# State space parameters made in the first stage, and the modulation's shift as a bias per column, in a hybrid S5 and gated DeltaNet block

## The chip, the cores and the metric

One core of a Trainium2 chip runs the whole kernel. The metric is the device time of one execution in microseconds (us), the median of several runs. The engines are named as in the profile: PE (TensorE), DVE (VectorE), ACT (ScalarE), POOL (GpSimd) and SP (SyncE), whose queue issues nearly all DMAs here.

## What is computed

The input x has 2048 tokens of 1024 columns. One conditioning vector c gives shift, scale and gate; the modulated and normalised h goes through one projection of 3088 columns, whose column groups feed a state space branch (u and z_a), a gated DeltaNet branch (q, k, v, z_b) and the DeltaNet's decay and step sizes (beta and alpha, called AB in the kernel).

```python
mod = silu(c) @ ada_w + ada_b
shift, scale, gate = split(mod, 3)
h = rms_norm(x, norm_w) * (1 + scale) + shift
u, z_a, qkv, z_b, beta, alpha = split(h @ w_in)
# state space branch: two directions, 32 groups of 64 states and 16 channels
dt = exp(log_step); mag = exp(lam_re * dt)
ab = mag * (cos(lam_im * dt), sin(lam_im * dt))   # one step of the recurrence
f = (ab - 1) / lam; bb = f * b                    # the input matrix
y_a = glu(gelu(scan(ab, bb, c, u) + d * u)) * silu(z_a)
# DeltaNet branch: convolution of five taps, chunks, two directions
y_b = norm(delta(silu(conv(qkv)), beta, alpha)) * silu(z_b)
out = rms_norm(x + gate * (concat(y_a, y_b) @ w_out))
```

What depends on lam and log_step alone (the powers of ab, f, and the turning factors of the scan) needs neither the input matrix b nor the output matrix c of the state space; those are the parameters of which the title speaks.

## The kernel before

**Numbers.** The projection runs in fp16 with split operands: each weight tile is scaled by a power of two and cut in a high half wh and a low half wl, h likewise in hhi and hlo, and a gemm of one tile of 128 columns by 512 tokens is 24 matmuls (eight slices k of the 1024 rows, in each hi by hi, hi by lo, lo by hi). `w_max` finds a weight tile's scale (squares on ACT, a sum over partitions by one matmul), `w_cut` applies it (three small operations on the DVE, wh on ACT, wl on the DVE). PSUM has eight banks: two named gm for gemms, three named pt and three named sq for turned (transposed) h and for small sums.

**First stage** (lines 250 to 497, an order written by hand). It loads x in four blocks of 512 tokens and the modulation's weights ada_w, makes h and the four tiles of u, and the gate. Loads go through SP's one queue in program order: c, ada_b, norm_w, the first weights (ws), x, then ada_w. The DVE sums the modulation (acc, with slices aw of ada_w), a matmul with ones (`mod_sum`) finishes it: first for the scale, later for the shift, last for the gate (accg). For a block, `x_square` (ACT), `x_root` (DVE) and `x_scale` normalise x, `h_turn` turns a slice k of it on PE into a bank, and `h_part` makes h of it:

```python
A.activation(out=hf, in_=src, func=AF.Identity, scale=aS[:, k:k + 1], bias=shS[:, k:k + 1])
P.tensor_scalar(out=hhi[:, k, sl], in0=hf, scalar1=1.0, scalar2=1.0, op0=ALU.mult, op1=ALU.mult)
V.tensor_tensor(out=hlo[:, k, sl], in0=hf, in1=hhi[:, k, sl], op=ALU.subtract)
```

Since the shift is known late, h of block 0 is first made without it, with a scale of its own (s_0, ih0); a chain of 96 matmuls of one column then multiplies the shift with the u weights (ub), and u of block 0 gets this as a bias. Blocks 1 to 3 wait for the shift, and h of block 0 is made again with the shift during block 3, for the later jobs. Block by block, four gemms (`u_out`, ct = 0 to 3) go with the work for the next block: scaling after the first, h after the third and fourth.

**Job stage.** The other 21 column tiles are jobs in a fixed order (`order`): three tiles of z_a, AB, K, Q, then V mixed with the rest. A job has four ticks (AB one), in each the gemm of one block, what leaves the bank (Silu for z, a copy into raw for the convolutions), a piece of the next job's `w_max` and `w_cut`, delayed work by ticks (`later`: the taps of the convolution, squares, turns) and one step of the generator `side`. That generator is the state space branch: parameters (`s5_params`, 9 steps), tables of input and output matrices per group (24), a reordering through DRAM, turning factors, the main loop over 16 batches (33), and the opening of the GLU: 85 steps in all, over the 81 ticks and some more at the end. The parameters are rows loaded by DMA, turned on PE, then some 250 small operations on the DVE (exponential, sine and cosine, the f, powers by doubling, squares, and the tables rtA and rtB) and a product with b on POOL.

**DeltaNet stages.** After the jobs comes the DeltaNet in two stages with the GLU beside it and the output projection at the end, in an order written by hand. The change doesn't touch them.

## Time and profile before

| what | value |
|---|---|
| median of 3 runs | 1407.08 us (1400.67 to 1408.08) |
| the profiled execution, its own time | 1399.43 us |
| its span | 1397.7 us |
| mean granted PE clock | 0.963 of full speed |
| first gemm starts | 40.18 us |
| block 2's first gemm starts | 112.25 us |
| job 4, the first of the job stage, starts | 165.66 us |
| end of the job stage, start of DeltaNet and GLU | about 770 us |

A row of the timeline reads: start in us, duration in us, engine, line, operation, written tile and read tiles, sizes, how many alike, and in brackets the idle time ahead of it on this engine with what ended it. A row of a table by windows reads: the window, its length, then for PE, PEld (weight loads), DVE, ACT and POOL the busy time with the count of instructions, then the granted PE clock, the busy share of the DMA engines and GB/s. A row of the waits reads: engine, tile and line, what it waited for, then total us, how often, the longest.

### The profile page before, as it was taken

Reading aid. Unit: us, or ns where it says so; the run is one execution under the profiler, and the core shown is the slowest. Engines: PE = TensorE matmul, PEld = TensorE weight load, DVE = VectorE, ACT = ScalarE, POOL = GpSimd, SP = SyncE. Lnnn points to the kernel's source line nnn. Section 1 sums busy time; section 2 is a strip of 40 time slices with the busy share of each in tenths; the row PEclk is TensorE's granted clock in tenths of the full one; section 3 lists DMA queues with packets and bytes.
Section 4 is the critical chain, followed back from the end, with each engine's and each line's share of the span. In section 5 each row is a group of like instructions: output and inputs, shape, how many; then the busy total and the mean of one; then the engine's idle time right before and its main releaser. Section 6 shows DMA issues by size and latency. Waiting matters only on the chain.

```text
span 1397.7 us, 26524 instructions
## 1 busy us (share of the span) xinstructions
PE 1282.3 (92%) x9936; PEld 900.3 (64%) x9936; DVE 1017.6 (73%) x2095; ACT 672.5 (48%) x1348; POOL 708.1 (51%) x680
## 2 busy tenths in 40 slices
PE   2879897898999999999999699999999988998997
PEld 2445343355665555555554588999998877887885
DVE  4635579877765899998984667888878655865664
ACT  4445322444655454354445566776667423432332
POOL 3214223656540477878840766666553235654443
PEclk9789999999999999999999899999999999999998
DMA  9446343223457434343524533544335488686533
GB/s 308 173 86 187 92 87 87 64 82 89 121 163 191 132 106 129 99 143 95 156 80 135 163 83 96 175 144 143 115 132 184 150 294 279 223 312 211 181 107 112
DMA packets 255280, 206.43 MB, mean 148 GB/s; under 512 B 88496, under 2 KB 206256, under 8 KB 255152
## 3 DMA queue, kind: packets, MB, share of 16 engines
q1 hardware_dynamic: 255152, 204.75, 47.3%
q8 instruction: 78, 1.28, 0.4%
q14 instruction: 50, 0.41, 0.1%
HBM read 133.38 MB, written 73.33 MB: 148 GB/s over the span
## 4 chain that ended last, share of the span: by engine, by line
PE 67%; DVE 16%; DMA 4%; issue 3%; POOL 3%; ACT 2%; SPq 1%; DVEq 0%; POOLq 0%; ACTq 0%
PE gm L33 37%; PE sq L33 15%; PE pt L33 12%; DVE sq L1033 2%; DVE w L510 2%; DVE tm L510 1%; DVE xs L939 1%; PE pt L1077 1%; POOL w L510 1%; DMA y<-ya_d 1%; DVE t L510 1%; PE sq L1750 1%; DMA xt<-in_x_dram 0%; DVE r L1782 0%; DVE cv L1033 0%
## 5 line engine op out<-in xcount | busy, mean ns | idle before, releaser
L33 PE MATMUL gm<-hhi,wh 128*128 128x512 f16 (+1 forms) x784 | 294.4, 390 | 13.4 <-ACT wh L221 6.9
L33 PE MATMUL gm<-hhi,wl 128*128 128x512 f16 (+1 forms) x784 | 293.1, 388 | 8.2 <-DVE wl L223 8.2
L33 PE MATMUL gm<-hlo,wh 128*128 128x512 f16 (+1 forms) x784 | 293.4, 389 | 0.0
L33 PEld LDWEIGHTS <-wh 128*128 128x128 f16 (+1 forms) x1664 | 154.0, 100 | 199.7 <-issue 26.0
L33 PEld LDWEIGHTS <-wl 128*128 128x128 f16 (+1 forms) x832 | 79.8, 100 | 106.1 <-DVE wl L223 10.7
L1017 ACT ACTIVATE raw<-gm,w 128x512 f32<-128x512 f32 x48 | 33.1, 689 | 175.9 <-PE gm L33 175.9
L510 POOL TENSOR_TENSOR w<-w,w 128x512 f32<-128x512 f32 x32 | 50.2, 1578 | 87.9 <-DVE w L510 87.9
L33 PE MATMUL gm<-yh,gwh 128*128 128x256 f32 x256 | 80.0, 313 | 6.7 <-ACT yh L778 5.6
L1033 DVE SCALAR_TENSOR_TENSOR sq<-raw,cw,cv 128x512 f32<-128x512 f32 x48 | 55.2, 1151 | 29.6 <-ACT cv L1025 29.5
L1033 DVE SCALAR_TENSOR_TENSOR sq<-raw,cw,sq 128x512 f32<-128x512 f32 x96 | 72.6, 756 | 3.4
L33 PE MATMUL gm<-yl,gwh 128*128 128x256 f32 x256 | 73.3, 286 | 0.7 <-POOL yl L779 0.7
L1772 POOL TENSOR_TENSOR r<-r,xt 128x512 f32<-128x512 f32 x32 | 41.5, 1297 | 62.9 <-DVE r L1771 29.2
L33 PE MATMUL gm<-yh,gwl 128*128 128x256 f32 x256 | 72.5, 283 | 0.0
L1442 ACT ACTIVATE Y<-pt 128x512 f16<-128x512 f32 x96 | 58.0, 604 | 23.9 <-PE pt L33 23.2
L33 PE MATMUL sq<-S,kq 128*128 128x128 f32 x480 | 62.3, 281 | 0.0
L939 DVE TENSOR_TENSOR_SCAN xs<-c,w 128x255 f32<-128x255 f32 x64 | 61.1, 1013 | 1.1 <-POOL w L510 1.1
L33 PEld LDWEIGHTS sq<-S,kq 128*128 128x128 f32 x480 | 59.9, 196 | 2.0
L1421 DVE CAST_PREDICATED pb<-msk,pt 128x512 f16<-128x512 int8 x80 | 56.9, 714 | 5.5 <-PE pt L33 4.4
L1003 ACT ACTIVATE z<-gm,w 128x512 f32<-128x512 f32 x32 | 22.0, 688 | 80.0 <-PE gm L33 48.0
L33 PE MATMUL pt<-Y,nh 128*128 128x64 f16 (+1 forms) x896 | 56.3, 198 | 4.5 <-DVE Y L1429 4.2
L320 POOL TENSOR_SCALAR hhi<-hf 128x512 f16<-128x512 f32 x32 | 30.1, 960 | 54.9 <-ACT hf L318 47.9
L1443 ACT ACTIVATE YT<-pt 128x512 f16<-128x512 f32 x96 | 57.3, 597 | 0.0
(455 smaller groups left out, 3544.9 us busy)
## 6 DMA issues: line engine op xcount, KB each, us to landing
xt<-in_x_dram SPq DMA_DIRECT2D x25, 512.0 KB
ws<-in_w_in_dram SPq DMA_DIRECT2D x24, 512.0 KB
aw<-in_ada_w_dram SPq DMA_DIRECT2D x24, 512.0 KB
kq<-kT_d SPq DMA_DIRECT2D x32, 256.0 KB
kq<-qT_d SPq DMA_DIRECT2D x32, 256.0 KB
kt<-kt_d SPq DMA_DIRECT2D x32, 256.0 KB
vt<-vt_d SPq DMA_DIRECT2D x32, 256.0 KB
out_dram<-r SPq DMA_DIRECT2D x16, 512.0 KB
```

Source lines behind the costliest of these rows:

```text
L33: nc.tensor.matmul(out, lhsT, rhs, start=start, stop=stop)
L320: P.tensor_scalar(out=hhi[:, k, sl], in0=hf, scalar1=1.0, scalar2=1.0, op0=ALU.mult, op1=ALU.mult)
L510: (e or V).tensor_tensor(out=o, in0=a, in1=b, op=op)
L939: V.tensor_tensor_scan(out=o, data0=m1, data1=v, initial=0.0, op0=ALU.mult, op1=ALU.add)
L1003: A.activation(out=z, in_=ps, func=AF.Silu, scale=iv)
L1017: A.activation(out=raw[:, 2 + tb * 512:2 + (tb + 1) * 512], in_=ps, func=AF.Copy, scale=iv)
L1033: V.scalar_tensor_tensor(out=cv if j == 4 else ps, in0=raw[:, o + j:o + j + 512], scalar=cw[:, i12, j:j + 1], in1=cv if j == 1 else ps, op ...
L1077: nc.tensor.transpose(ps[:, j * 128:(j + 1) * 128], cv[:, j * 128:(j + 1) * 128], ident)
L1421: V.copy_predicated(out=cols(PB[d][li], b, d), mask=mb, data=pp.rearrange("p t (n b) -> p t n b", b=b))
L1442: A.activation(out=cols(Y[d], b, d), in_=pa.rearrange("p t (n b) -> p t n b", b=b), func=AF.Copy)
L1443: A.activation(out=cols(YT[d], b, 1 - d), in_=pb.rearrange("p t (n b) -> p t n b", b=b), func=AF.Copy)
L1772: P.tensor_tensor(out=r[:, ns], in0=r[:, ns], in1=xt[:, ns], op=ALU.add)
```

## The change

Two things change together.

**Parameters early.** A generator `s5_early` holds what of `s5_params` needs neither b nor c. Its first step, six DMAs, stands at the very front of SP's queue; its next two (two transposes, two copies, both exponentials) stand between `w_max(0)` and `w_cut(0)`, ahead of everything else of the first stage. The other ten steps stand in the loop over the blocks, one after the gemms ct = 0 and 3, two after ct = 1 and 2: sine, cosine, f, powers and squares in block 1, what is left of the squares, the exchange by DMA and rtB in block 2, rtA in block 3. Powers and f go to DRAM (pw_d, cf_d), and `s5_params` loads them again; it has four steps instead of nine, so `side` has 80 instead of 85.

**Shift as bias.** h is made without the shift in all blocks, with one scale, from the bank in two operations; block 0 is not made again. The shift gets its own scale (ish), and every tile of columns its bias: `w_bias`, 24 matmuls of one column (96 with 16 columns of weights for AB) into a pt bank and a copy by ACT, at the job's start (for the u tiles, behind the gemm (1, 1)). The bias is added by the instruction that leaves the gemm's bank. Six tiles of u that are finished before the shift (block 0, and two of block 1) are kept in xk and get it on POOL (`u_add`). Block 2 is squared and scaled earlier, and mod_sum for the shift comes behind five u gemms instead of in the fourth.

```diff
@@ s5_early, new; its steps are those of s5_params, moved
+    def s5_early(sc_):
+        for src in ((lam_re_f, lam_re_b), (lam_im_f, lam_im_b)):
+            rows = sc_.tile([NG, 128], F32, tag="rows", name="rows", bufs=2)
+            for d in range(2):
+                nc.sync.dma_start(out=rows[:, d * 64:d * 64 + 64], in_=src[d][0])
+            raws.append(rows)
+        for d, a in enumerate((log_step_f, log_step_b)):
+            nc.sync.dma_start(out=dt[d * 64:d * 64 + 64], in_=a.to_broadcast([64, NG]))
+        yield
...
+        exp_acc(dt, dt)
+        yield
+        TT(th, li, dt, ALU.mult)
+        TT(t0, lr, dt, ALU.mult)
+        exp_acc(mag, t0)
+        yield
+        sincos(cu, su, th)
+        yield
...
+        nc.sync.dma_start(out=pw_d, in_=pwt)
+        nc.sync.dma_start(out=cf_d, in_=cf)
@@ first stage
+        par = s5_early(p0.enter_context(pool("ke", side="right")))
+        next(par)
...
         whole(w_max(0))
+        for _ in range(2):
+            next(par)
         whole(w_cut(0))
@@ h_part
-            A.activation(out=hf, in_=src, func=AF.Identity, scale=aS[:, k:k + 1], bias=shS[:, k:k + 1])
-            P.tensor_scalar(out=hhi[:, k, sl], in0=hf, scalar1=1.0, scalar2=1.0, op0=ALU.mult, op1=ALU.mult)
-            V.tensor_tensor(out=hlo[:, k, sl], in0=hf, in1=hhi[:, k, sl], op=ALU.subtract)
+            A.activation(out=hhi[:, k, sl], in_=src, func=AF.Copy, scale=aS[:, k:k + 1])
+            V.scalar_tensor_tensor(out=hlo[:, k, sl], in0=src, scalar=aS[:, k:k + 1], in1=hhi[:, k, sl],
+                                   op0=ALU.mult, op1=ALU.subtract)
@@ w_bias, new
+    def w_bias(w, n, rows=(0,)):
+        ps = bank("pt")
+        for k in range(KT):
+            for a, b, j in ((0, 0, 0), (0, 1, 1), (1, 0, 2)):
+                for r in rows:
+                    mm(nc, ps[r:r + n, 0:1], w[a][:, k, :], sh[b][:, k:k + 1], k + j == 0, k == KT - 1 and j == 2)
+        wb = sp.tile([128, 1], F32, tag="wb", name="wb", bufs=NU)
+        for r in rows:
+            A.activation(out=wb[r:r + n], in_=ps[r:r + n, 0:1], func=AF.Copy, scale=w[3][r:r + n])
+        return wb
@@ u_add, new
+        def u_add(b, ct):
+            ur = raws.pop((b, ct))
+            P.tensor_scalar(out=ur, in0=ur, scalar1=ub[ct], scalar2=1.0, op0=ALU.add, op1=ALU.mult)
+            u_store(b, ct, ur)
@@ the loop over the blocks
-                u_out(b, ct, gemm(uw[ct], b), uw[ct][2])
+                if b > 1 or ct > 1:
+                    u_out(b, ct, gemm(wprep[ct], b), ub[ct])
+                for _ in range(2 if ct in (1, 2) else 1):
+                    next(par, None)
...
-                elif ct < 2:
-                    for k in range(4 * ct, 4 * ct + 4):
-                        h_part(0, k, xk[:, k])
@@ s5_params
+        pw = kp.tile([128, 2, T + 1, NG], F32, name="pw")
+        nc.sync.dma_start(out=pw, in_=pw_d)
+        cf = kp.tile([128, 4, NG], F32, name="cf")
+        nc.sync.dma_start(out=cf, in_=cf_d)
@@ job
-        w = w_done(i)
+        w = wprep[i]
+        wb = w_bias(w, 128)
         for tb in range(NB):
             ps = gemm(w, tb)
-            evac(tb, ps, w[2])
+            evac(tb, ps, w[2], wb)
```

How the change moves instructions, at three places. The first is the start of the program on the DVE; w_240 to w_242 are the scale of the first weights, e and eki the temporaries of the exponential, dt and mag its two results. Before:

```order
L74 MEMSET ones 128x128
L143 TENSOR_SCALAR w_216<-pt 128x1
L145 TENSOR_SCALAR w_217<-w_216 128x1
L147 TENSOR_SCALAR w_218<-w_216 128x1
L223 SCALAR_TENSOR_TENSOR wl<-ws,w_217,wh 128x1024
L104 CAST gtr<-gt 128x128
L104 CAST ltr<-lt 128x128
L299 TENSOR_SCALAR ss<-ss 128x4
```

The same place after the change, from the end of the second exponential on:

```order
L317 TENSOR_SCALAR eki<-e_289 128x32
L318 TENSOR_SCALAR eki<-eki 128x32
L266 TENSOR_TENSOR e_291<-e_291,eki 128x32
L320 SCALAR_TENSOR_TENSOR mag<-t_260,e_291 128x32
L143 TENSOR_SCALAR w_240<-pt 128x1
L145 TENSOR_SCALAR w_241<-w_240 128x1
L147 TENSOR_SCALAR w_242<-w_240 128x1
L227 SCALAR_TENSOR_TENSOR wl<-ws,w_241,wh 128x1024
L503 TENSOR_SCALAR ss<-ss 128x4
```

Both casts, the copies of two turned rows and 38 operations of the exponentials now stand ahead of the first scale, which stood second in the queue.

The second is PE at the same place, after the change; rows are the loaded rows of lambda, w_239 the squares' sum of the first weights:

```order
L33 MATMUL pt<-w_239,ones 128x1
L296 MATMUL pt<-ident,rows 128x32 x2
L517 MATMUL pt<-ident,xt 128x128 x4
L517 MATMUL sq<-ident,xt 128x128 x4
L517 MATMUL pt<-ident,xt 128x128 x4
```

The two transposes of the rows stand behind the sum over the first weights; in the old kernel the transposes of x follow on that sum at once.

The third is the DVE in block 2, between the scaling of block 3 (xt) and block 3's low halves (hlo). Before:

```order
L120 SCALAR_TENSOR_TENSOR rs<-rxt,rxy 128x4
L307 TENSOR_SCALAR xt<-xt,rs 128x1024 x4
L277 TENSOR_SCALAR accg<-aw,sc 128x1024
L279 SCALAR_TENSOR_TENSOR accg<-aw,sc,accg 128x1024 x2
L321 TENSOR_TENSOR hlo<-hf,hhi 128x512 x12
```

After, the last of the rows that stand between the gate's sum and hlo (cu and su are a sine and a cosine being squared, rtB the table, tp temporaries):

```order
L266 TENSOR_TENSOR tp_1438<-rtB_163,cu 128x256
L266 TENSOR_TENSOR rtB_162<-tp_1435,tp_1436 128x32x8
L266 TENSOR_TENSOR rtB_163<-tp_1437,tp_1438 128x32x8
L266 TENSOR_TENSOR t_260<-cu 128x32
L266 TENSOR_TENSOR t_261<-su 128x32
L266 TENSOR_TENSOR den<-cu,su 128x32
L266 TENSOR_TENSOR cu<-t_260,t_261 128x32
L393 TENSOR_SCALAR su<-den 128x32
L266 TENSOR_TENSOR t_260<-cu 128x32
L266 TENSOR_TENSOR t_261<-su 128x32
L266 TENSOR_TENSOR t_260<-t_260,t_261 128x32
L397 TENSOR_SCALAR t_260<-t_260 128x32
```

Behind two more rows comes the first hlo of block 3. Seventy-four operations of the parameters stand between accg and it, and hlo reads the bank itself instead of hf.

More of the change, by code (lines that the diff above doesn't have):

```diff
@@ L173, in block @@
     ih = hpool.tile([128, 1], F32, name="ih")
+    ish = hpool.tile([128, 1], F32, name="ish")
+    sh = [hpool.tile([128, KT], F16, name=n) for n in ("shh", "shl")]
     cw = s5t.tile([128, 12, 5], F32, name="cw")
@@ L214, in w_cut @@
             return
[L215 removed]
+        ps, ma, s, iv, ib, wh, wl = wprep[i]
         ws = wraw[i]
@@ L247, in gemm, with TT, cmul @@
         return ps
+    rtA = [s5t.tile([128, NG, 8], F32, name=f"rtA{i}") for i in range(2)]
+    rtB = [s5t.tile([128, NG, 16], F32, name=f"rtB{i}") for i in range(2)]
+    c2 = s5t.tile([128, 5, NG], F32, name="c2")
+    def TT(o, a, b, op, e=None):
+        (e or V).tensor_tensor(out=o, in0=a, in1=b, op=op)
+    def cmul(o, a, b, shape, sc_, e=None):
+        t = [sc_.tile(shape, F32, tag=f"tp{i}", name=f"tp{i}", bufs=1) for i in range(4)]
+        TT(t[0], a[0], b[0], ALU.mult, e)
+        TT(t[1], a[1], b[1], ALU.mult, e)
+        TT(t[2], a[0], b[1], ALU.mult, e)
+        TT(t[3], a[1], b[0], ALU.mult, e)
+        TT(o[0], t[0], t[1], ALU.subtract, e)
+        TT(o[1], t[2], t[3], ALU.add, e)
@@ L384, in block @@
                 whole(w_max(2))
-        ss = x_square(x1)
-        first = []
-        iv0 = small("iv0", NU)
+        raws = {}
         def shift_add(*ks):
@@ L404, in block @@
             x_scale(x1, rs, j, (A, P)[j % 2])
-        next(cuts[3])
-        next(cuts[3])
+        u_raw(0, 1)
+        whole(mx)
+        whole(cuts[3])
+        turns = ("pt", "sq")
+        u_raw(0, 2)
+        shift_add(0, 1)
+        for k in range(0, 4):
+            h_part(1, k, h_turn(x1, k, turns[k % 2]))
         shift_add(2, 3)
-        whole(cuts[3])
+        u_raw(0, 3)
+        for k in range(4, KT):
+            h_part(1, k, h_turn(x1, k, turns[k % 2]))
+        xs_ = {2: x_load(2)}
         shift_add(4, 5)
@@ L413, in block @@
         P.tensor_tensor(out=aws[6], in0=aws[6], in1=aws[7], op=ALU.add)
-        first.append(gemm(wprep[2], 0, "sq"))
-        turned = [h_turn(x1, k, t) for k, t in enumerate(("pt", "pt", "sq"))]
-        first.append(bank("sq"))
-        gemm_part(first[3], wprep[3], 0, range(4))
+        u_raw(1, 0)
+        ss = x_square(xs_[2])
         mod_sum(0, [acc, aws[6]])
-        gemm_part(first[3], wprep[3], 0, range(4, KT))
-        xs_ = {2: x_load(2)}
+        rs = x_root(ss)
+        for j in range(4):
+            x_scale(xs_[2], rs, j, V)
@@ L453, in block @@
-        for ct in range(NU):
-            u_out(0, ct, first[ct], iv0[:, ct:ct + 1], bias=ub[:, ct:ct + 1])
+            ib = wprep[ct][3]
+            V.tensor_tensor(out=ib, in0=ib, in1=ish, op=ALU.mult)
+            ub.append(w_bias(wprep[ct], 128))
+        for b, ct in ((0, 0), (0, 1), (0, 2), (0, 3), (1, 0), (1, 1)):
+            u_add(b, ct)
         pada.close()
@@ L541, in s5_params @@
         yield
-        for rows, dst in zip(raws, (lr, li)):
-            ps = bank("pt")
-            nc.tensor.transpose(ps[:, 0:NG], rows, ident[0:NG, 0:NG])
-            V.tensor_copy(out=dst, in_=ps[:, 0:NG])
-        yield
         cr, nci = [kp.tile([128, NG, SN], F32, name=n) for n in ("cr", "nci")]
@@ L679, in s5_params @@
-        pk = kp.tile([128, 2, 5, NG // 2], F32, name="pk")
-        def keep(i, t):
-            V.tensor_copy(out=pk[:, :, i], in_=t.rearrange("p (r j) -> p j r", j=2))
-        n = 1
-        magT = k32("magT")
-        src = mag
-        while n < T:
-            if 2 * n == T:
-                keep(2, cu)
-                keep(3, su)
-            square()
-            TT(magT, src, src, ALU.mult)
-            src = magT
-            n *= 2
-        for i, t in ((0, cu), (1, su), (4, magT)):
-            keep(i, t)
@@ L1000, in z_job, with evac @@
     def z_job(i, dst):
-        def evac(tb, ps, iv):
+        def evac(tb, ps, iv, wb):
             z = tp.tile([128, 512], F32, tag="z", name="z", bufs=3)
-            A.activation(out=z, in_=ps, func=AF.Silu, scale=iv)
+            A.activation(out=z, in_=ps, func=AF.Silu, scale=iv, bias=wb)
             nc.sync.dma_start(out=dst[:, tb * 512:(tb + 1) * 512], in_=z)
@@ L1101, in ab_job @@
     def ab_job(i):
-        wh, wl, iv = w_done(i)
+        wh, wl, iv = wprep[i][0:3]
+        wb = w_bias(wprep[i], 16, [32 * j for j in range(NB)])
         ps = bank("gm")
```

387 lines of the change are left out of this document (188 added, 199 removed).

## The prediction, made before the changed kernel ran

> **What bounds the kernel now.** First the page's line of busy times, then the busy time by stage (a row per stretch of time in us, with the granted clock behind the engines), then the PE's waits in the two stages that the change touches, then the timelines around those waits.
>
> ```profile
> PE 1282.3 (92%) x9936; PEld 900.3 (64%) x9936; DVE 1017.6 (73%) x2095; ACT 672.5 (48%) x1348; POOL 708.1 (51%) x680
> ```
>
> ```profile
> 0.00:40.00 40.00, 9.20 (x54) 8.04 (x55) 20.53 (x45) 21.45 (x34) 12.67 (x32) 0.90 0.93 321
> 40.00:78.00 38.00, 36.01 (x252) 20.09 (x252) 21.80 (x44) 14.98 (x22) 11.50 (x10) 0.83 0.30 106
> 78.00:112.00 34.00, 27.35 (x134) 14.14 (x135) 14.84 (x39) 15.66 (x26) 7.62 (x9) 0.85 0.66 169
> 112.00:166.00 54.00, 49.37 (x236) 24.17 (x235) 34.57 (x54) 25.03 (x39) 19.97 (x20) 0.97 0.42 114
> 166.00:296.00 130.00, 113.99 (x690) 54.31 (x687) 102.56 (x341) 38.58 (x79) 51.86 (x50) 0.93 0.32 83
> ...
> 486.00:760.00 274.00, 269.62 (x1497) 143.66 (x1498) 240.44 (x308) 135.44 (x211) 187.48 (x153) 0.99 0.39 118
> ```
>
> The PE is the bound nearly everywhere: from 486 to 760 it is busy 98% of the time, so every matmul added there counts in full. It is not the bound in the first 40 us (the front: no gemm yet), in 78 to 112 (6.65 us idle), and in the start of the job stage, 166 to 296 (16 us idle, with the DVE busy 79% and 341 instructions on it). A change to the state space parameters and to the shift acts in just these places. All sums below are against the profiled execution (1399.43 us, span 1397.7); the median of the runs shown is 7.65 us higher, and the sum is carried over to it at the end.
>
> **The front: later by 12.1 us.** The parameters' first three steps now stand ahead of everything that leads to the first gemm. The old front, in order of time:
>
> ```profile
> 10.01 0.16 DVE L143 TENSOR_SCALAR w<-pt 128x1 int32<-128x1 int32 x1 [8.96 <-PE pt L33]
> ...
> 10.39 1.15 ACT L221 ACTIVATE wh<-ws,w 128x1024 f16<-128x1024 f32 x1 [1.06 <-DVE w L145]
> ...
> 39.73 0.59 PE L33 MATMUL pt<-w,ones 128*128 128x1 f32 x2 [7.57 <-ACT wl L203]
> ```
>
> The DVE makes the scale of the first weights at 10.01, ACT waits for it with wh, and behind wh on ACT stand the squares of x, on which the roots, the modulation and the first gemm (right behind the 39.73 row) hang. Now the DVE comes to w only after 38 small operations, and those come after two transposes that PE holds behind the weights' sum (the order above), so they don't run beside the load but after it. What these steps cost in their old place:
>
> ```profile
> 172.66 0.64 SPq L519 DMA_DIRECT2D rows<-in_lam_re_f_dram  x1
> ...
> 175.34 0.59 SPq L522 DMA_DIRECT2D dt<-in_log_step_b_dram  x1
> ...
> 178.96 0.18 DVE L562 TENSOR_SCALAR e<-dt 128x32 f32<-128x32 f32 x1 [0.59 <-DMA dt<-in_log_step_b_dram]
> ...
> 182.61 0.19 DVE L579 SCALAR_TENSOR_TENSOR dt<-dt,e 128x32 f32<-128x32 f32 x1
> ```
>
> Six issues on SP from 172.66 to 175.93: 3.3 us by which all later loads start later. One exponential, 18 operations, takes 178.96 to 182.80, 0.213 us apiece. Two of them and th, t0 are 38 operations: 38 x 0.213 = 8.1 us. Two transposes and copies, about 0.7 us (an estimate: four operations of two engines at that size). Sum 12.1. Bounds: 8.8, if the DMA issues are hidden because the first weights' load wasn't what ACT waited for; 14, with waits between the steps. I take 12.1: nothing stands in that chain that was waiting for something else. No cover is left behind which it could hide.
>
> **Block 1, without the wait for the shift: earlier by 4.6 us.** The two largest waits of the first stage, PE's, 40 to 166:
>
> ```profile
> PE pt L33 <- ACT wl L203: 12.2, 2, 7.6
> PE gm L33 <- ACT u L449: 6.5, 1, 6.5
> ```
>
> The second is the wait of block 1's first gemm for a bank that ACT empties behind the h parts with the shift. After it PE runs slowly for a while:
>
> ```profile
> 85.74 0.61 PE L33 MATMUL gm<-hhi,wh 128*128 128x512 f16 x1 [6.48 <-ACT u L449]
> ...
> 93.12 0.38 PE L33 MATMUL gm<-hhi,wh 128*128 128x512 f16 x1
> ...
> 98.30 0.38 PE L33 MATMUL gm<-hhi,wh 128*128 128x512 f16 x1
> ```
>
> The gemm behind the wait takes 7.38 us, the next 5.18: each such wait costs 2.2 us more. With the shift kept out, block 1's h needs the scale alone, and 6.5 + 2.2 = 8.7 us go. What comes late instead: the bias chain needs the shift's fp16 halves, which the DVE makes after scaling block 2; PE then waits some 2.1 us (an estimate: squares of block 2 on ACT 4.9, root 2.3, scaling 2.7 and shift 2.9 are one chain of 12.8 us, against 4 us of PE for the modulation and a slow gemm of 7.4, so 1.4; and 0.7 for the first hlo of block 2). Then 2 us for the lock told next. Net -4.6; bounds -8.7 and +1.
>
> Sincos, f and the powers run right after, on the DVE, while POOL adds the bias to six U tiles. What that does is seen in the old job stage:
>
> ```profile
> 200.01 1.11 POOL L510 TENSOR_TENSOR tp<-bbr,f_im 128x512 f32<-128x512 f32 x1
> ```
>
> ```profile
> 200.11 1.05 DVE L510 TENSOR_TENSOR tm<-pwi 128x32 f32<-128x32 f32 x1
> 201.09 0.18 DVE L510 TENSOR_TENSOR tm<-pwr,pwi 128x32 f32<-128x32 f32 x1
> ```
>
> The same small operation takes 1.05 us where a POOL operation runs, and ends with it, and 0.18 otherwise. Six additions of about 1 us can so add 0 to 5.2 us (6 x 0.87) to the DVE's steps ahead of block 2's hlo; I take 2, since only part of it reaches PE. The Trainium skill (SBUF — State Buffer, "Who interferes with whom") states it as an exclusive lock: a DVE instruction with two SBUF inputs and a GpSimd instruction that reads SBUF shut each other out for the whole instruction. By that rule nearly every step here would meet one POOL instruction, and the term would be its upper end, 5.2 instead of 2, the sum 3 us higher.
>
> **Blocks 2 and 3: later by 9.7 us.** Ahead of block 3's hlo the DVE now has, behind the scaling and the gate's three additions, 74 operations more (rtB in four steps). Squaring, in its old place, where nothing contends:
>
> ```profile
> 213.42 0.19 DVE L510 TENSOR_TENSOR t<-cu 128x32 f32<-128x32 f32 x1
> ...
> 215.06 0.18 DVE L510 TENSOR_TENSOR magT<-magT 128x32 f32<-128x32 f32 x1
> ```
>
> 1.65 us for a square of 11, so 0.15 apiece: four squares 6.6, four products of growing width (24 operations) 4.8, copies and signs 1: 12.4 us. The old place of block 3's first hlo:
>
> ```profile
> 131.56 3.72 DVE L321 TENSOR_TENSOR hlo<-hf,hhi 128x512 f16<-128x512 f32 x4
> ```
>
> That is 19.3 us after block 2's first gemm (at 112.25, where the fourth stage of the table begins), straight behind scaling and gate, so with rtB ahead of it 31.7. PE has by then done four gemms and six turns (four gemms of 5.18 and six turns of 0.44: 23.4) and stands: h turns into six banks, and a bank comes free only when hlo has read it, where the old ACT copy hf freed it at once. That is about 8 us idle and the 2.2 us of slow clock behind it. The 4.6 of the first waits row (12.2 less 7.6), for the next weights behind the remade block 0 on ACT, shrinks to about 2: -2.5, but the two copies of rtA among block 3's h cost about 2 again. Sum 8 + 2.2 - 2.5 + 2 = 9.7; bounds 0 and 15.
>
> **Start of the job stage: earlier by 17.3 us.** PE's waits, 166 to 296:
>
> ```profile
> PE gm L33 <- DVE wl L223: 8.2, 3, 5.1
> PE gm L33 <- ACT wh L221: 6.9, 2, 6.0
> ```
>
> The next job's weights are cut on the DVE in its queue behind parameters, many of them slowed by POOL as shown. Some 250 of the DVE's 341 operations go. I let 13.3 of these 15.1 us go (the last 1.8 are two waits at a later job, when the parameters are long made), and 2.2 us of slow clock behind each of the two long ones: 17.7. New: the rows of C are wanted one tick earlier than before, behind two reloads on SP, where a wait of PE for the rows of lambda goes; the difference about 0.4 us. Net -17.3; bounds -19 and -8 (if the tables' products on POOL, now five ticks earlier, hold the DVE up in the parameters' stead).
>
> **The bias chains: 13.5 us more PE.** Every job begins with 24 matmuls of one column. The old chain of 96:
>
> ```profile
> 72.34 0.21 PE L33 MATMUL pt<-shh,wh 128*128 128x1 f16 x1
> ...
> 74.84 0.64 PE L313 MATMUL pt<-ident,xt 128*128 128x128 f32 x4
> ```
>
> 2.50 us for 96, 26 ns each, weight loads of 128 columns among them: 0.63 us a job. Nineteen jobs (job 4's is in the stage above) 12.0, and 96 of 16 columns in AB about 1.5. Bounds 9 (some of it in waits that remain) and 18. A rule of the Trainium skill speaks against the change here (TensorE: Matmul & The Clock Gate, "LDWEIGHTS (loading the stationary operand)"): a load takes its columns over 1.2 in ns, 107 ns for 128, and each of these matmuls has its own; were they to follow each other, the term would be 24 x 107 ns x 19 = 49 us and the sum 35 higher. The 26 ns of the trace say that they overlap.
>
> **Side work five steps earlier: earlier by 2.5 us.** The side steps need 80 ticks instead of 85. The state space main loop so begins beside denser convolutions, where the DVE has 88% already (240.44 of 274): +4 (0 to 10; where a pair of ticks has more DVE than PE work, PE waits). And at the end of the stage:
>
> ```profile
> 772.82 0.58 PE L33 MATMUL gm<-yh,gwh 128*128 128x256 f32 x1 [4.82 <-ACT yh L778]
> ```
>
> This wait for the first GLU rows falls away, as their load and cast come some ticks ahead: 4.8, and 1.7 of slower clock and small waits behind it: -6.5 (bounds -3 and -8).
>
> **Sum.** 12.1 - 4.6 + 9.7 - 17.3 + 13.5 - 2.5 = +10.9: 1410 us for the profiled execution, and 1407.1 + 10.9 = 1418 for the median.
>
> **Rivals.**
> - Faster: the DVE has room. Then hlo of block 3 comes before PE runs out of banks (the point: all steps ahead of it done within 23.5 us of block 2's first gemm, not 31.7), no dense tick is late, and the lock reaches nobody: 9.7, 2 and 4 fall away, the job stage gains its bound, the bias chains hide a little (12): 12.1 - 6.6 - 19 + 12 - 6.5 = -8: 1399. For it: the DVE is busy 34.57 of 54 us there. Against it: that room lies ahead of the root, where the steps can't go.
> - The stalls stay: it is POOL, not the parameters, that makes the DVE late with wl, and the tables bring POOL's products five ticks earlier into the same jobs. -17.3 becomes -8: 1427.
> - Denser: the main loop meets convolutions that fill the DVE, +10 instead of +4, and the lock takes its upper end: 1427 too, told apart by where PE waits (486 to 760 instead of 166 to 296).
> - The weight loads of the bias chains follow each other: 1453. The 26 ns speak against it.
>
> **How the numbers follow.** Forecast 0.46, with an own range of 1408 to 1428, and of it a third under 1414; room on the DVE 0.25, over half of it under 1400; stalls stay 0.13; denser 0.13; loads 0.03. Half a per cent (1400.0 and 1414.1 here) is about what a measurement of this kernel can tell from no change. Under 1400: 0.15 of the second case and 0.01 of the first; within: 0.15 of the first, 0.10 of the second, 0.05 of the others' lower ends; above: the rest. The range 1397 to 1431 leaves out the loads and the far ends of the last two and of the second, less than 2 in 10.
>
> **What would show it.** The first gemm at about 52.3 us; block 1's gemm without its 6.5 us wait; between block 2 and 3 a PE wait of some 8 us for the DVE; no PE wait over 3 us for wl or wh from job 5 on; 24 bias matmuls in 0.6 us at each job's start; the GLU's first wait gone. I am wrong if the first gemm comes before 49, if PE doesn't stand ahead of block 3, or if bias chains take over 1 us.

## The result, and the profile after

The changed kernel takes 1437.33 us (median of 4 runs, 1434.73 to 1438.17) where the kernel before takes 1404.58 (median of 4): a ratio of 1.0229, with 1.0205 to 1.0253 as its 95% interval. It is slower by 32.8 us; 10.9 were forecast. The sign is right, and the time lies outside the range.

The profiled execution took 1437.84 us, with a span of 1436.1. Against the span before, that is +38.4, more than the medians differ, since the profiled execution before (1399.43 us) lies 5.2 under that kernel's median. The line of busy times of the changed kernel:

```profile
PE 1305.4 (91%) x10512; PEld 920.5 (64%) x10512; DVE 989.4 (69%) x2107; ACT 680.4 (47%) x1370; POOL 672.5 (47%) x654
```

PE is busy 23 us longer (more matmuls, and a slower clock in places) and the span is 38 longer, so 15 us of new idle time stand somewhere, while the DVE is even busy 28 us less. To find the place, both runs are cut at the same pieces of work (start of the first gemm, of block 2's first, of job 4's bias or gemm, of the jobs Q2 and V3, and the end of the last job's gemm):

| stretch | before, us | after, us | difference |
|---|---|---|---|
| start to the first gemm | 0 to 40.18 | 0 to 51.31 | +11.1 |
| to block 2's first gemm | to 112.25 | to 115.85 | -7.5 |
| to job 4 | to 165.66 | to 178.87 | +9.6 |
| to job Q2 | to 431.9 | to 440.45 | -4.7 |
| to job V3 | to 689.6 | to 736.3 | +38.2 |
| to the last job's end | to 766.6 | to 805.3 | -8.0 |
| the rest | | | -0.3 |

The busy time of the changed kernel in the same stretches (columns as in the table by windows of the prediction):

```profile
0.00:51.00 51.00, 9.63 (x55) 8.32 (x55) 28.16 (x85) 21.40 (x34) 12.65 (x32) 0.93 0.74 252
51.00:116.00 65.00, 63.03 (x389) 34.29 (x390) 46.74 (x170) 30.33 (x51) 12.36 (x12) 0.87 0.33 95
116.00:179.00 63.00, 50.59 (x237) 24.60 (x234) 45.32 (x187) 18.97 (x30) 0.00 (x0) 0.89 0.57 162
179.00:441.00 262.00, 252.70 (x1931) 140.33 (x1928) 137.29 (x265) 118.81 (x242) 128.62 (x128) 0.97 0.43 117
441.00:737.00 296.00, 273.80 (x1689) 152.48 (x1687) 259.17 (x338) 133.77 (x217) 191.01 (x164) 0.96 0.36 108
```

And the kernel before, from job 4 to Q2 and from Q2 to V3:

```profile
166.00:432.00 266.00, 245.20 (x1583) 132.72 (x1581) 198.26 (x520) 109.31 (x224) 127.02 (x128) 0.96 0.38 102
432.00:690.00 258.00, 253.55 (x1435) 137.94 (x1434) 233.50 (x306) 124.40 (x205) 177.98 (x149) 0.99 0.44 130
```

The loss lies between Q2 and V3. There PE idles 22.2 us (296 less 273.80) against 4.45 before: 17.8 more. Its granted clock is 0.96 against 0.99, worth about 8 of its 273.8 us. Eight bias chains of 0.61 take 4.9. What is left, some 7 us, is put down here to side work that stood behind V3 before: PE has 254 matmuls more in this stretch, 192 of them the chains', and the next stretch is 8.0 us shorter. So about 26 us are lost where 4 were forecast. The first four stretches came out nearly as told; their rows follow.

The front, on the DVE, ACT and PE, in order of time:

```profile
12.97 0.19 DVE L297 COPY lr<-pt 128x32 f32<-128x32 f32 x1 [9.84 <-PE pt L296]
...
21.14 0.15 DVE L143 TENSOR_SCALAR w<-pt 128x1 int32<-128x1 int32 x1
...
21.51 1.15 ACT L225 ACTIVATE wh<-ws,w 128x1024 f16<-128x1024 f32 x1 [9.46 <-DVE w L145]
...
50.86 0.59 PE L33 MATMUL pt<-w,ones 128*128 128x1 f32 x2 [7.58 <-ACT wl L206]
```

The scale of the first weights is made at 21.14 instead of 10.01: 2.96 us until the first turned row is copied (12.97), 8.17 for what stands between. All of these 11.1 us reach the first gemm, at 51.31.

PE's waits from the first gemm to job 4, and the largest of them where it happens (7.6 of the second row belong to the front):

```profile
PE pt L517 <- DVE hlo L523: 9.9, 1, 9.9
PE pt L33 <- ACT wl L206: 9.5, 2, 7.6
PE pt L33 <- DVE shh L659: 1.6, 1, 1.6
```

```profile
150.25 0.47 PE L517 MATMUL pt<-ident,xt 128*128 128x128 f32 x1 [9.94 <-DVE hlo L523]
```

Block 1's wait of 6.5 is gone, the shift's halves cost 1.6 where 2.1 was forecast for them and the first hlo of block 2 together, and PE stands 9.9 us (until 150.25) for the first hlo of block 3, where 8 was forecast. From job 4 on the waits for weights shrink to

```profile
PE pt L747 <- DMA crows<-in_c_re_b_dram: 2.6, 1, 2.6
PE pt L33 <- DVE wl L227: 2.0, 1, 2.0
...
PE pt L33 <- ACT wh L225: 0.7, 1, 0.7
```

against 8.2 and 6.9 before. What comes later was not foreseen. PE's waits between 440 and 740 in the changed kernel:

```profile
PE sq L33 <- DVE cv L1076: 13.4, 3, 5.5
PE pt L1137 <- DVE kt L1130: 5.1, 1, 5.1
PE pt L33 <- DVE wl L227: 3.4, 3, 1.9
```

and the largest of them in the kernel before, between 486 and 760:

```profile
PE sq L33 <- DVE cv L1033: 2.0, 2, 1.2
```

The waiting matmuls (line 33 into sq) are those of the state space main loop; cv is the last of a convolution's four operations on the DVE.

### The profile page after: what moved, and what is told of

The parts are those of the page before. It is cut to its first block, busy times and chain, and to the rows that moved or that the text cites. A ratio compares the mean times of both kernels' runs of the same rounds, so it can differ in the third digit from the quotient of the medians.

```text
span 1436.1 us, 27667 instructions
## 1 busy us (share of the span) xinstructions
PE 1305.4 (91%) x10512; PEld 920.5 (64%) x10512; DVE 989.4 (69%) x2107; ACT 680.4 (47%) x1370; POOL 672.5 (47%) x654
## 4 chain that ended last, share of the span: by engine, by line
PE 63%; DVE 16%; DMA 3%; ACT 2%; issue 2%; POOL 1%; SPq 0%; DVEq 0%; ACTq 0%; POOLq 0%
PE gm L33 34%; PE sq L33 15%; PE pt L33 12%; DVE sq L1076 4%; DVE w L266 4%; DVE xs L981 2%; DMA y<-ya_d 1%; DVE wl L227 1%; DVE cv L1076 1%; PE pt L1120 1%; DMA of<-o_d 1%; DVE YT L1478 1%; DVE pb L1465 1%; PE sq L1794 0%; PE sq L880 0%
## 5 line engine op out<-in xcount | busy, mean ns | idle before, releaser
L33 PE MATMUL gm<-hhi,wh 128*128 128x512 f16 (+1 forms) x800 | 302.5, 389 | 0.0
L33 PE MATMUL gm<-hlo,wh 128*128 128x512 f16 (+1 forms) x800 | 302.0, 389 | 0.0
L33 PE MATMUL gm<-hhi,wl 128*128 128x512 f16 (+1 forms) x800 | 300.6, 387 | 0.0
L33 PEld LDWEIGHTS <-wh 128*128 128x128 f16 (+1 forms) x2048 | 167.6, 99 | 193.1 <-issue 32.8
L33 PEld LDWEIGHTS <-wl 128*128 128x128 f16 (+1 forms) x1024 | 93.5, 99 | 102.4 <-issue 9.1
L1060 ACT ACTIVATE raw<-gm,wb,w 128x512 f32<-128x512 f32 x48 | 37.4, 779 | 177.3 <-PE gm L33 173.7
L1046 ACT ACTIVATE z<-gm,wb,w 128x512 f32<-128x512 f32 x32 | 24.9, 778 | 121.4 <-issue 74.3
L821 POOL TENSOR_TENSOR yl<-yf,yh 128x256 fp32r<-128x256 f32 x32 | 27.9, 873 | 111.9 <-ACT wb L243 59.1
L227 DVE SCALAR_TENSOR_TENSOR wl<-ws,w,wh 128x1024 f16<-128x1024 f32 (+1 forms) x25 | 42.3, 1693 | 51.9 <-ACT wh L225 51.9
L266 DVE TENSOR_TENSOR w<-sq,rt 128x512 f32<-128x512 f32 x64 | 40.5, 684 | 31.2 <-PE sq L33 31.2
```

Source lines behind the costliest of these rows:

```text
L33: nc.tensor.matmul(out, lhsT, rhs, start=start, stop=stop)
L227: V.scalar_tensor_tensor(out=wl, in0=ws, scalar=s, in1=wh, op0=ALU.mult, op1=ALU.subtract)
L266: (e or V).tensor_tensor(out=o, in0=a, in1=b, op=op)
L821: P.tensor_tensor(out=nat(yl)[:, k], in0=yf[:, k], in1=nat(yh)[:, k].bitcast(F32), op=ALU.subtract)
L1046: A.activation(out=z, in_=ps, func=AF.Silu, scale=iv, bias=wb)
L1060: A.activation(out=raw[:, 2 + tb * 512:2 + (tb + 1) * 512], in_=ps, func=AF.Identity, scale=iv, bias=wb)
```

## Where the wait comes from

The main loop works in pairs of ticks. In the first, called the in-tick here, PE multiplies a batch's inputs (16 matmuls into sq) and the DVE takes four products of them. In the second, the out-tick, come the output matmuls, and four scans, two products and a sum on the DVE, some 8 us. Beside them runs a job of four ticks. A V job's four convolutions fall in its ticks 3 and 4 and in ticks 1 and 2 of the next job, and in a tick the convolution is put in the DVE's queue ahead of the side step. The side has 80 steps now instead of 85. Five is odd, and a pair has two ticks: from now on each in-tick meets the tick of a job where an out-tick stood before. The arrangement of the kernel before is called the old phase below, this one the flipped phase. First the DVE in the changed kernel, from an out-tick to the next in-tick:

```profile
636.15 3.66 DVE L981 TENSOR_TENSOR_SCAN xs<-c,w 128x255 f32<-128x255 f32 x4
639.74 2.82 DVE L266 TENSOR_TENSOR w<-xs,rt 128x512 f32<-128x512 f32 x2
642.59 1.64 DVE L266 TENSOR_TENSOR w<-w,w 128x512 f32<-128x512 f32 x1
644.15 1.75 DVE L1076 SCALAR_TENSOR_TENSOR sq<-raw,cw,cv 128x512 f32<-128x512 f32 x1
...
647.52 0.75 DVE L1076 SCALAR_TENSOR_TENSOR cv<-raw,cw,sq 128x512 f32<-128x512 f32 x1
650.35 0.69 DVE L266 TENSOR_TENSOR w<-sq,rt 128x512 f32<-128x512 f32 x1 [2.08 <-PE sq L33]
```

The in-tick's matmuls on PE at that place:

```profile
648.33 3.31 PE L33 MATMUL sq<-uT,bpt 128*64 128x256 f32 x16 [5.50 <-DVE cv L1076]
```

The last convolution of the job stands behind the scans, begins at 644.15, ends at 648.27, and PE starts 0.06 us later, after 5.5 us of waiting. Then the DVE waits for PE in its turn (2.08), and the next gemm stands behind these matmuls in PE's queue. In the kernel before, the same convolution comes in an out-tick, ahead of the scans:

```profile
605.80 0.79 DVE L1033 SCALAR_TENSOR_TENSOR sq<-raw,cw,cv 128x512 f32<-128x512 f32 x1
...
608.87 3.67 DVE L939 TENSOR_TENSOR_SCAN xs<-c,w 128x255 f32<-128x255 f32 x4
...
618.03 2.47 DVE L510 TENSOR_TENSOR w<-sq,rt 128x512 f32<-128x512 f32 x4
```

The matmuls of the following in-tick:

```profile
615.08 1.95 PE L33 MATMUL sq<-uT,bpt 128*64 128x256 f32 x16
```

They are on PE at 615.08, before the DVE wants their product (618.03): nobody waits, and the 16 take 1.95 us instead of 3.31.

## The experiments

Three theories were held against each other. A, the amount: the main loop starts five ticks earlier and meets denser work, so each tick that it is held back brings back its share. B, the phase: only odd or even counts. C, the chains: the bias chains cost far more than 13.5 us. After them come kernels on the other terms of the sum. All differences are between medians, against the kernel before on the same chip in the same set.

| kernel | median, us | before, us | ratio (95% interval) | difference |
|---|---|---|---|---|
| the change | 1437.33 | 1404.58 | 1.0229 (1.0205 to 1.0253) | +32.8 |
| yield1 | 1413.70 | 1405.95 | 1.0052 (1.0032 to 1.0072) | +7.8 |
| yield4 | 1439.00 | 1405.95 | 1.0237 (1.0211 to 1.0263) | +33.1 |
| yield5 | 1421.36 | 1405.95 | 1.0110 (1.0089 to 1.0130) | +15.4 |
| nochain | 1431.26 | 1405.95 | 1.0186 (1.0161 to 1.0211) | +25.3 |
| before_plus1 | 1424.56 | 1405.62 | 1.0137 (1.0115 to 1.0158) | +18.9 |
| y1_front | 1404.13 | 1405.62 | 0.9995 (0.9978 to 1.0012) | -1.5 |
| y1_b2 | 1411.34 | 1405.62 | 1.0042 (1.0025 to 1.0058) | +5.7 |
| y1_nochain | 1397.89 | 1405.62 | 0.9939 (0.9917 to 0.9962) | -7.7 |
| best1 | 1394.51 | 1404.47 | 0.9924 (0.9905 to 0.9943) | -10.0 |
| shift_alone | 1413.35 | 1404.47 | 1.0067 (1.0046 to 1.0087) | +8.9 |
| params_alone | 1412.83 | 1404.47 | 1.0053 (1.0033 to 1.0074) | +8.4 |
| in_first | 1421.26 | 1406.20 | 1.0086 (1.0052 to 1.0119) | +15.1 |

### Empty side steps: yield5, yield1, yield4

The changed kernel with n empty steps in `s5_side`, behind the four steps of the parameters; n is 5, 1 and 4:

```diff
             yield
+        for _ in range(n):
+            yield
         last = iter(())
```

> The changed kernel with five empty side steps between the state space parameters and the tables, so that tables, reordering and main loop meet the same ticks of the jobs as before the change. Theory A (the side work that now runs earlier packs the main loop's DVE work into the convolution jobs, PE waits for the DVE): the 33 us lost between Q2 and V3 come back and the 10.6 us won in the last jobs go: about 1415 us, no PE wait over 2 us on a convolution's bank. Theory B (it is the phase: a shift by an odd count of ticks flips which half of a main loop batch meets which tick of a job): the same, 1415, since five is odd. Theory C (the bias chains with their waits cost the jobs far more than 0.63 us each, the shift of the side work little): 1430 to 1437.

> The same with one empty step: tables and main loop come four ticks earlier than before the change, but in the old phase within a batch. A: one of five steps given back, about 1432. B: the old phase is enough, 1413 to 1420. C: 1435 to 1437.

> The same with four empty steps: only one tick earlier than before the change, in the flipped phase. A: four of five steps given back, about 1420. B: the flipped phase keeps most of the loss, 1430 to 1440. C: 1430 to 1437.

One empty step takes the loss from 32.8 to 7.8 us, four leave it at 33.1, five bring 15.4. By the amount, four steps would have given nearly what five give. So B holds, though yield5 came out 6 us above the 1415 that A and B both gave for it. In yield1 the stretch from Q2 to V3 takes 273.7 us (438.27 to 711.99) instead of 295.9. PE's waits in the late jobs, 440 to 760, first in yield1 and then in yield4:

```profile
PE sq L33 <- DVE cv L1076: 1.9, 2, 1.0
```

```profile
PE sq L33 <- DVE cv L1076: 16.7, 3, 5.6
PE pt L33 <- DVE wl L227: 6.1, 5, 2.0
```

The amount, that is the earlier start, has a part of its own, and with the other sign than forecast: in the old phase, starting four ticks earlier (yield1 against yield5) is 7.7 us faster, not slower. In the flipped phase it gives nothing (0 against 4 steps: 0.3). What the 7.7 are made of was not followed up.

### The flip without the change: before_plus1

The kernel before, with one empty step after its nine steps of the parameters:

```diff
             yield
+        yield
         last = iter(())
```

> The kernel before the change with nothing but one empty side step behind the state space parameters. If the phase of the main loop against the jobs is what costs (theory B, now the leading one), the old kernel loses about what the changed one lost by it, 20 to 27 us: 1425 to 1433, with PE waits of 4 us and more for the convolution in the V jobs. If the phase only hurts together with the bias chains or the earlier start, it stays at 1404 to 1410.

+18.9 us, from one empty step. PE's waits from 430 to 760:

```profile
PE sq L33 <- DVE cv L1033: 17.0, 3, 6.5
PE gm L33 <- DVE wl L223: 4.7, 4, 2.8
```

These are the waits of the changed kernel, with none of its edits. Most of the loss is thus no property of early parameters or of a bias, but of a step count with the other parity. It is of the size of yield4 less yield5 (17.6). The step counts with this loss are 80, 84 and, here, 86; those without it are 81 and 85. Counts that leave three when divided by four, the ticks of a job, were not run: that they would do as well as 81 and 85 follows from the pairs of ticks and is not shown.

### The side step ahead of the convolution: in_first

The changed kernel in its flipped phase; in in-ticks the side step now goes ahead of the delayed work:

```diff
+        turned = BATS and clock[0] % 2 == BATS[0] % 2
+        if turned:
+            next(side, None)
         for e in sorted((e for e in late if e[0] <= clock[0]), key=lambda e: e[2]):
             late.remove(e)
             e[1]()
-        next(side, None)
+        if not turned:
+            next(side, None)
...
+            if not BATS:
+                BATS.append(clock[0])
             next(turn, None)
```

> The changed kernel in its own, flipped phase (no empty step); in the ticks in which a batch of the main loop enters (its 16 matmuls and the four products that read them) that step is put ahead of the tick's convolution instead of behind it. If the flipped phase costs because the batch's matmuls wait for a convolution that is queued on the DVE behind the previous tick's scans, the waits for the convolution (13.4 us) go with their slow clock: 1412 to 1425. If the DVE simply has more than PE to do in these pairs of ticks, the waits come back at the next matmul that needs the DVE: 1431 or more.

+15.1 instead of +32.8. The waits for cv are gone from the list; what is left between 440 and 780 is led by

```profile
PE pt L1142 <- DVE w L143: 5.8, 1, 5.8
PE pt L33 <- DVE wl L227: 2.3, 4, 0.8
```

So about 18 of the 25 us that the old phase is worth hung on the order of these two pieces in one tick. In the rest are the other waits of that phase, such as the one for w. One thing stays open: why PE's matmuls wait for just that convolution. A convolution keeps its sum in one of the three sq banks, which the main loop uses too; the banks go round, and their turn alone doesn't give the wait; a kernel in which the convolution uses another bank was not tried.

### The bias chains: nochain and y1_nochain

The 20 chains of the jobs and that of AB are left out; the instruction that leaves the bank still adds a bias, that of a u tile. nochain is the changed kernel with this edit, y1_nochain is yield1 with it.

```diff
         w = wprep[i]
-        wb = w_bias(w, 128)
+        wb = ub[i % NU]
...
-        wb = w_bias(wprep[i], 16, [32 * j for j in range(NB)])
+        wb = ub[0]
```

> The changed kernel without the bias chains of the 21 jobs: it leaves out their matmuls and puts the bias of a u tile in the place of each job's own, so the instruction that leaves the bank is the same. A and B: 20 chains at 0.65 us and AB's go, 12 to 15 us, so 1422 to 1425, and the waits for the convolutions' banks between Q2 and V3 stay. C: 25 us or more go, 1412 or less, and those waits go with them.

> The changed kernel with one empty step and without the bias chains of the 21 jobs; it leaves out their matmuls and uses the bias of a u tile in their place. If a chain costs what its matmuls take on a bound PE (0.65 us a job, AB 2.7), 13 to 16 us go: 1398 to 1401. If much of it lies in waits that PE has at the jobs' starts anyway, as the 6 us in the flipped phase suggest: 1405 to 1409.

C falls: without its chains the changed kernel is still 25.3 us slower. They cost 7.5 us there, less than the 12 to 15 expected, and 15.5 in the old phase (+7.8 against -7.7). That PE waits anyway in the flipped phase would explain the difference; no run shows it by itself. The 15.5 is the price of 20 chains and AB's, where the prediction had 12.0 for nineteen and 1.5 for AB; job 4's it put into another term, whose sum doesn't show it. In the trace of the changed kernel a chain takes 0.61 us and AB's 0.73 (254.67 to 255.40), 12.9 for all; the 2.6 above that were not followed up. The Trainium skill's rule (TensorE: Matmul & The Clock Gate, "LDWEIGHTS (loading the stationary operand)", 107 ns for 128 columns), taken as a price for each of these matmuls, would have made it 51 us for 20 chains. The measurement decides for the 26 ns of the old trace: there a load's record lasts about 0.10 us and the next one starts 0.026 later, so the loads overlap.

### Other places for the early steps: y1_front and y1_b2

Both are yield1 with another placement. y1_front puts the six DMAs behind the loads of ada_w, and the two steps of exponentials ahead of the roots of blocks 1 and 2:

```diff
-        next(par)
         ap_ = pada.enter_context(pool("ada", side="right"))
...
         aws = [aw_load(av_, D, k) for k in range(6)]
+        next(par)
         whole(w_max(0))
-        for _ in range(2):
-            next(par)
         whole(w_cut(0))
...
         next(mx)
+        next(par)
         rs = x_root(ss)
...
         mod_sum(0, [acc, aws[6]])
+        next(par)
         rs = x_root(ss)
```

> The changed kernel with one empty step (1413.7 us), and its first three parameter steps moved: the six DMAs behind the loads of the first block, one exponential ahead of block 1's roots, one ahead of block 2's. Theory: the front's delay lies wholly on the path, the first gemm comes at 40 to 41 us instead of 51, and 10 to 11 us go: 1403. Rival: the first stage then waits for the same things later (the roots behind the exponentials), 5 us or less go: 1408 or more.

The first gemm stands at

```profile
41.49 0.59 PE L33 MATMUL gm<-hhi,wh 128*128 128x512 f16 x1
```

9.8 us earlier than in the changed kernel, and by the medians 9.2 of them reach the end (+7.8 to -1.5). The front was a real term on the path, and no more than a matter of place.

y1_b2 moves rtB and the first step of rtA from ahead of block 3's h to behind it. (Behind its first three steps `s5_early` has fourteen more, not ten: the squares all stand in block 1, the exchange, rtB and the first step of rtA in block 2.)

```diff
-                for _ in range(2 if ct in (1, 2) else 1):
+                for _ in range((1, 0, 0, 0)[ct] if b == 2 else 2 if ct in (1, 2) else 1):
                     next(par, None)
...
+                if b == 2 and ct == 3:
+                    for _ in range(5):
+                        next(par)
```

> The changed kernel with one empty step, and the four steps of rtB with the first of rtA put behind block 3's h instead of ahead of it. Theory: the 9.9 us wait of PE between blocks 2 and 3 goes with 2 us of slow clock behind it: 1402 to 1404. Rival: the steps then make the weights of job 4 late, and half of it comes back there: 1407 or more.

The 9.9 us wait is gone, yet by the medians only 2.0 us reach the end, and the intervals of yield1 and y1_b2 overlap. PE's waits from 51 to 200 show one part of where the rest went:

```profile
...
PE pt L33 <- DVE accg L483: 3.8, 1, 3.8
PE pt L750 <- DMA crows<-in_c_re_b_dram: 3.0, 1, 3.0
```

The gate's sum (accg) now stands on the DVE behind the moved steps, a new wait of 3.8. The wait for the rows of C is no part of it: yield1 has the same 3.0. The other part is the clock in job 4. That job starts 4.7 us earlier than in yield1 (173.77 against 178.43), but takes 31.7 us against 27.5, at a granted clock of 0.79 (173 to 206) against 0.94 (178 to 206), so that job 5 starts only 0.5 earlier. A stall that is taken away in one place uncovers what was late behind it.

### The halves alone: shift_alone and params_alone

shift_alone keeps the parameters in the job stage (the old `s5_params`, 85 steps) and takes over only the shift as bias; against the changed kernel:

```diff
-        par = s5_early(p0.enter_context(pool("ke", side="right")))
-        next(par)
...
-        for _ in range(2):
-            next(par)
...
-                for _ in range(2 if ct in (1, 2) else 1):
-                    next(par, None)
```

> Only the shift's part of the change: h without the shift and a bias per column, with the state space parameters in the job stage as before (85 side steps, old phase). From 1405.6: 15.8 for the bias chains, 4 to 9 off for block 1's wait and block 0's second h; the waits for weights at the start of the job stage stay: 1412 to 1418. Rival: without POOL and ACT work for h the first stage wins more than the chains cost: 1400 or less.

params_alone leaves the shift in h, with block 0 made again, and makes the parameters in the loop over the blocks, most of them at its end; hf and the u tiles have two buffers instead of four, and one empty step stands in `s5_side`, behind the first step of the parameters. Against the kernel before:

```diff
+                    for _ in range({(1, 0): 2, (1, 1): 1, (1, 3): 4, (2, 3): 1}.get((b, ct), 0)):
+                        next(par)
...
+        whole(par)
...
         par = s5_params(kp, sc_, st5)
+        next(par)
+        yield
+        yield
```

> Only the parameters' part: h with the shift as before, the parameters in the loop over the blocks (rtB and rtA behind it), none of them in the front, one empty side step for the phase; for room two buffers less each for hf and u. From 1405.6: the 15 us of waits for weights at the start of the job stage and their slow clock go, the DVE steps in the loop cost 0 to 5: 1388 to 1394, and no bias chains. Rival: the blocks wait for the DVE as in the changed kernel, or for the fewer buffers: 1400 or more.

Each half alone loses about as much as both together in the old phase: +8.9 and +8.4, against +7.8 (yield1). The first was expected at 1412 to 1418, as it came; the second at 1388 to 1394, 19 us and more below what it took. In shift_alone job 4 starts 10.6 us earlier than before (165.66),

```profile
155.06 0.17 PE L33 MATMUL pt<-shh,wh 128*128 128x1 f16 x1
```

but the waits for the weights at the jobs' start stay, behind the parameters on the DVE, and the chains come on top (15.5 us by y1_nochain). PE's waits from 155 to 300:

```profile
PE pt L33 <- DVE wl L227: 12.4, 3, 6.0
PE pt L33 <- ACT wh L225: 3.5, 2, 2.6
```

In params_alone the stalls move and grow. PE's largest waits from 40 to 300; all of them there add up to about 50 us, in the kernel before to 37:

```profile
PE pt L33 <- ACT wl L203: 16.2, 2, 8.8
PE gm L33 <- ACT wh L221: 13.3, 2, 11.6
```

Its smaller buffers may have a part in that; no kernel separated them from the moved steps.

### Put together: best1

The changed kernel with the front as in y1_front, an empty step between the first two of `s5_params`, three steps of rtB behind block 3's h, and the rest of rtB and rtA behind job 4's weights:

```diff
-                for _ in range(2 if ct in (1, 2) else 1):
-                    next(par, None)
+                for _ in range((2 if ct in (1, 2) else 1) if b == 1 else (1, 0, 0, 0)[ct] if b == 2 else 0):
+                    next(par)
...
+                if b == 2 and ct == 3:
+                    for _ in range(3):
+                        next(par)
...
         whole(par)
...
         par = s5_params(kp, sc_, st5)
+        next(par)
+        yield
+        yield
```

> The changed kernel with what the runs so far point to: one empty side step for the phase, put between the first and second step of the state space parameters (the rows of C so get a tick more); the exponentials out of the front; rtB behind block 3's h and rtA behind the weights of job 4. From 1413.7: 9.6 for the front, 8 to 12 for the wait between blocks 2 and 3, 2 to 3 for the rows of C: 1389 to 1394, below both kernels. Rival: the moved DVE steps make the next thing late, as in the last run with rtB moved alone, and only the front's part holds: 1400 to 1405.

1394.51 us, a ratio of 0.9924 (0.9905 to 0.9943): 0.8% below the kernel before, with an interval clear of 1, and just above the range expected. Job 4 starts at 156.46, 22.4 us earlier than in the changed kernel. And where that one lost its time, the window from 441 to 737 is now full:

```profile
441.00:737.00 296.00, 291.24 (x1813) 159.24 (x1810) 259.21 (x342) 146.75 (x235) 188.08 (x153) 0.99 0.39 116
```

The window holds somewhat later work, as the jobs begin earlier. The DVE has the same 259 us of work in it as in the changed kernel (259.17); PE does 124 matmuls more, at a clock of 0.99. yield1, which differs from the changed kernel by one empty step, already has 291.79 us of PE beside 259.37 of the DVE in that window. A DVE that is busy 88% is not what made PE wait; the order of its work is.

## Why the prediction was right in its sign and wrong in its size

| step | forecast | measured | by |
|---|---|---|---|
| front | +12.1 (8.8 to 14) | +11.1 | first gemm 51.31 against 40.18 |
| block 1 | -4.6 (-8.7 to +1) | -7.5 | first gemm to block 2's first |
| blocks 2 and 3 | +9.7 (0 to 15) | +9.6 | block 2 to job 4 |
| start of the job stage | -17.3 (-19 to -8) | about -14 | idle 20.8 to 9.3 us, clock 0.96 to 0.97 |
| bias chains | +13.5 (9 to 18) | +15.5 | y1_nochain against yield1 |
| denser main loop | +4 (0 to 10) | about +26 | idle and clock between Q2 and V3 |
| GLU boundary | -6.5 (-8 to -3) | -0.3 | the rest of the span |

- **Front, block 1, blocks 2 and 3.** The mechanisms were those told, and the sizes within the bounds. Block 1 was 2.9 us better. Two of the forecast's microseconds were for POOL's lock on the DVE; beside the six additions of U on POOL (102.53 to 106.66) the DVE's small operations took 0.35 to 0.63 us, several of them still 0.18, some 2.3 us more in all. None of it reached PE, which has no wait for an hlo of block 2. So the Trainium skill's exclusive lock (SBUF — State Buffer, "Who interferes with whom"), by which the term would have been 5.2, was not borne out at that size here: an addition took 0.69 us, not 1, and the six came in one run of 4.13 us that only some of the operations met.
- **Start of the job stage.** 11.5 us less idle, and about 2.5 from the clock. The rows of C took 2.6 where the rows of lambda had taken 0.8: 1.8 more, forecast at 0.4.
- **The failed step** is "Side work five steps earlier": "the state space main loop so begins beside denser convolutions, where the DVE has 88% already (240.44 of 274): +4 (0 to 10; where a pair of ticks has more DVE than PE work, PE waits)". It counted work per pair of ticks. That sum doesn't change when a pair is shifted by one tick; what changes is which half of it meets which half of the job. The step asked how dense the neighbours are, and had to ask whether five is odd. In place of the +4, PE idled 17.8 us more between Q2 and V3 and lost about 8 to its clock. yield1 (-25.0 us for one empty step), yield4 and before_plus1 show that it is the phase; starting four ticks earlier in the old phase is worth 7.7 us of gain.
- **GLU boundary.** The wait of 4.82 for the first GLU rows went, as told, but another came in its place, in the changed kernel at 812.83:

```profile
812.83 0.58 PE L33 MATMUL gm<-yh,gwh 128*128 128x256 f32 x1 [4.18 <-ACT sg L838]
```

ACT comes to sg late, behind a table load and the first pb copies of the DeltaNet:

```profile
808.62 1.28 ACT L1236 ACT_TABLE_LOAD   x1
...
810.40 2.01 ACT L1626 ACTIVATE pb<-id 128x1024 f16<-128x1024 f16 x2
...
812.30 0.48 ACT L838 ACTIVATE sg<-gm,glub 128x256 f32<-128x256 f32 x1
```

The prediction named what goes and didn't say what is late next.

- **The rivals.** "Denser" had the place (PE's waits between 486 and 760) and the sign, but not the cause or the size. "The stalls stay" and "loads follow each other" were wrong by the waits from 179 to 305 and by y1_nochain (and 49 us of loads in the place of 12.0 would be 37 more, not the 35 of the prediction). "The DVE has room" was wrong as the order was written; best1, with the steps where the room is, lands at 1394.5.

- **The signs.** All that the prediction named came about as told: the first gemm at 51.31, PE standing 9.9 us ahead of block 3, no wait over 2.0 for wl or wh from job 5 on, chains of 0.61 us. None of them watched the ticks in which the main loop runs.

Without the phase the forecast would have been near: +10.9 less the 4 for density is +6.9, and yield1 measured +7.8. That is in part luck, as two errors cancel in it: the GLU boundary gave nothing, and the earlier start gained.

## What to carry to other kernels

Where two streams of work with their own periods are woven into in-order queues, a change in the count of steps ahead of one of them shifts its phase for all that follows: look at the count modulo the period before anything else, and try one empty step on the kernel before, which prices the phase by itself. A sum of busy time per period says nothing about it, since both phases have the same sum. And before work is moved to an earlier stage, follow the chain to its first large instruction: here six loads, two transposes and 38 operations of 0.2 us cost 11 us at the front; with the loads behind those of the first block and the operations ahead of the roots of two later ones, about 2 by the medians.

## What the runs showed of the hardware that was not expected

An eviction of a bank by ACT takes longer when a bias per partition goes with it. The convolution's copy in the changed kernel, and then in the kernel before (busy us, mean ns behind the bar):

```profile
L1060 ACT ACTIVATE raw<-gm,wb,w 128x512 f32<-128x512 f32 x48 | 37.4, 779 | 177.3 <-PE gm L33 173.7
```

```profile
L1017 ACT ACTIVATE raw<-gm,w 128x512 f32<-128x512 f32 x48 | 33.1, 689 | 175.9 <-PE gm L33 175.9
```

That is 90 ns for each of 48. It should cost little here, as ACT waits for PE before nearly all of them (173.7 us in all). The operation was changed with it (a copy before, an identity with bias now). The z tiles, where it is Silu with a scale in both kernels and the bias alone is new, show that it is the bias, 778 ns against 688:

```profile
L1046 ACT ACTIVATE z<-gm,wb,w 128x512 f32<-128x512 f32 x32 | 24.9, 778 | 121.4 <-issue 74.3
```

```profile
L1003 ACT ACTIVATE z<-gm,w 128x512 f32<-128x512 f32 x32 | 22.0, 688 | 80.0 <-PE gm L33 48.0
```

A product of one column on the DVE can take as long as what POOL is at. In the changed kernel:

```profile
653.92 1.07 DVE L222 TENSOR_TENSOR w<-w,ish 128x1 f32<-128x1 f32 x1
```

It ends at 654.99, with the second of two POOL products (654.97); in the kernel before, the like operation at 199.93, just as a POOL instruction ended (at 200.05), took 0.16. Not every small operation beside POOL is held: some of those between 102.53 and 106.66 took 0.18, as told above.
